# A gated-DeltaNet decoder trunk: where the next head's decays are traced, and weight operations in halves

## The chip, the cores and the metric

The kernel runs on one core of a Trainium2 chip. The core has a matrix engine (TensorE, PE in the profile; PEld is its weight load), a vector engine (VectorE, DVE), an activation engine (ScalarE, ACT), a general engine (GpSimd, POOL), and a sync engine (SP) that here only issues DMAs. Each works through its own queue in order, and semaphores tie the queues together. The metric is the device time of one execution in microseconds.

## The reference

The model has two layers over a sequence of 1024 tokens of width 1024. The first is a gated DeltaNet with 8 heads, the second a sliding-window attention. The change concerns the first layer's heads and the weights of both layers. For each head, in chunks:

```python
q, k, v = ...            # projection, causal convolution of 4 taps, SiLU; q and k normed
g = cumsum(log-decay)    # within a chunk
decay = exp(where(tri, g[c] - g[s], -inf))
lower = where(strict, beta * (k k^T) * decay, 0)
u, w = solve(I + lower, [v * beta, k * beta * exp(g)])
qk = (q k^T) * decay
for each chunk:          # the recurrence, S is 128 x 256
    v_new = u - w S
    o = (q * exp(g)) S + qk v_new
    S = S * exp(g_last) + (k * exp(g_last - g))^T v_new
```

Then o is normed and gated with SiLU(z) and projected by `a_w_out`; a shared K/V projection, the attention layer and its output projection follow. All weights are float32, and norm factors are vectors of length 1024 that multiply the normed input; in the second layer the kernel multiplies them into the weight rows.

## The kernel before

Every product with a weight is made from three products of a faster 32-bit type: a weight block of 128x1024 values is loaded into `wraw`, `whi` is its rounded value, `wlo` = `wraw` - `whi`, and the input is split in the same way into `hh` and `hl`. `weight` (L138) makes 146 of the 148 blocks (two are made apart in `weight_first`), with the subtraction on DVE (L152). For the weights without a norm factor `whi` comes from POOL (L148); for the 36 with one (K/V and the second layer's input weights) POOL first multiplies the raw block by the factor in place (L150) and ACT makes `whi` (L151). `gemm_ct` (L169) runs 24 matmuls per block and half of the tokens (L175, L177, L179).

The first layer goes head by head, with chunks of 128. `head_in(h)` is the projection of one head: k, q and two blocks of v, each in two halves (`ConvBlock.half`), with a SiLU and its sink behind each half. `head_delta(h)` is the head's own chain: the products of keys and queries (L660) with the decays `dm`, an inverse of the triangular matrix by levels of doubling (L716, L720), two corrections in full precision, a merge that ends in the copy of the last quarter into `xt` (ACT, L761), and then the recurrence over the 8 chunks. A chunk of the recurrence has: the product with the state (L787), the row r (DVE, L789), the product with the inverse (PE, L796), its high part (ACT, L798, tile `Z`) and low part (DVE, L799, tile `lh`), the state's update (PE, L807 to L810; DVE, L813), and the state's high part (ACT, L818, tile `X`) and low part (DVE, L819).

`interleave` (L86) runs the chain of head h and, in its gaps, the projection of head h+1 and the gate of head h. This fixes the order of PE, which runs as traced. On the other engines a planner orders the instructions: it issues what is ready, in the order of the trace where several are, so an instruction whose inputs come early can run well ahead of its place in the trace. `keep_in_program_order` ties an instruction to the one traced ahead of it on its engine.

The decays of a head are loaded (`decays_load`, L598), masked on POOL (`decays`, L603) and put through eight exponentials of 128x128 on ACT (L607). `dm` has one buffer for even heads and one for odd heads. The mask and the first exponential are marked with `keep_in_program_order`; the other seven are not. In `head_in`, decays of heads 1 to 7 are traced one tick behind the first half of the first v block; head 0 starts on its own and has them behind the first half of the second. ACT holds one set of function tables at a time; the exponential and SiLU are in different sets, and a table load stands in its queue at each change.

Of the kernel before, what the change touches and what calls it, by code (L numbers as in the profile page):

```python
# [13 lines left out]
ALU = mybir.AluOpType  # L14
# [4 lines left out]
P = 128  # L19
# [45 lines left out]
class Kernel:  # L65
# [72 lines left out]
    def weight(self, src, shape, gain=None):  # L138

        nc = self.nc  # L140
        pool = self.wpools[self.wcount % len(self.wpools)]
        self.wcount += 1
        view = lambda t: t.rearrange("p (k c) -> p k c", k=shape[0])
        raw = self.weight_load(src, shape)
        hi = view(pool.tile([P, 1024], F32R, name="whi"))
        lo = view(pool.tile([P, 1024], F32R, name="wlo"))
        if gain is None:
            nc.gpsimd.tensor_scalar(out=hi, in0=raw, scalar1=1.0, scalar2=1.0, op0=ALU.mult, op1=ALU.mult)  # L148
        else:
            nc.gpsimd.tensor_tensor(out=raw, in0=raw, in1=gain.unsqueeze(2).broadcast_to([P] + shape), op=ALU.mult)  # L150
            nc.scalar.copy(out=hi, in_=raw)  # L151
        nc.vector.tensor_tensor(out=lo, in0=raw, in1=self.f32(hi), op=ALU.subtract)  # L152
        return hi, lo

    def fetch(self):
# [455 lines left out]
    def head_in(self, h, started=None):  # L611
        if started is None:
            k, q, v_sink = self.head_blocks(h)
            self.head_tiles(h)
            H = self.nxt
            self.decays_load(h, H)
            for half in range(2):
                yield from k.half(half)
            for half in range(2):
                yield from q.half(half)  # L620
        else:
            k, q, v_sink = started
            H = self.nxt
        v = [None, None]
        for vb in range(2):
            v[vb] = self.ConvBlock(self, 16 + 2 * h + vb, v_sink(vb))
            for half in range(2):
                yield from v[vb].half(half)
                if (vb, half) == ((0, 0) if started is None else (1, 0)):
                    if started is not None:  # L630
                        self.later(1, lambda: self.decays_load(h, H))
                    self.later(1, lambda: self.decays(h, H))
        self.cur = H

# [761 lines left out]
```

## Time and profile before

| | |
|---|---|
| median of 3 runs | 1904.08 us (1901.43 to 1906.32) |
| profiled execution | 1903.49 us, of which the span is 1901.7 us |
| PE busy | 1831.0 us, 96% of the span |
| DVE busy | 1232.2 us, 65% |
| ACT busy | 813.6 us, 43% |
| POOL busy | 517.1 us, 27% |
| first layer's heads | about 104 to 855 us |
| its output projection | about 855 to 1095 us |
| second layer with attention | about 1095 to 1750 us |
| its output projection | about 1750 to 1902 us |

The profiled execution is the one that all rows come from. A row of the timeline gives the start, the length, engine, line, operation, output<-input and, in brackets, how long the engine sat idle before it and for what. Matmul ends are modelled, so PE's busy time doesn't say how close PE is to its peak; what counts is where it idles and for whom.

### The profile page before, as it was taken

The numbers are of one execution on the slowest core, as the hardware profiler recorded it, in microseconds if no ns is written. First come the engines' busy times: TensorE is split into PE (matmuls) and PEld (weight loads), VectorE is DVE, ScalarE is ACT, GpSimd is POOL, SyncE is SP. The second block draws the span as 40 slices with busy tenths as digits, with TensorE's granted clock in tenths as the row PEclk, the third lists the DMA queues.
The fourth block names the chain that finished last, engine by engine and source line by source line (L and its number), as shares of the span: only waits on it lengthen the run. The fifth ranks groups of instructions, "written<-read, shape, count | busy, mean of one in ns | idle before, by whom it ended". The sixth has DMA issues, their size and how long they took to land.

```text
span 1901.7 us, 33658 instructions
## 1 busy us (share of the span) xinstructions
PE 1831.0 (96%) x13186; PEld 1566.8 (82%) x13186; DVE 1232.2 (65%) x2868; ACT 813.6 (43%) x1948; POOL 517.1 (27%) x545
## 2 busy tenths in 40 slices
PE   6999999999999998999999999999999999999999
PEld 6677777787878776778999998888788788879999
DVE  6677766768585878765445266787786686753432
ACT  6446353535334353523112043557756656771100
POOL 0332222323232223220211222333433333321111
PEclk9999999999999999999999999999999999999999
DMA  4611111111111111122654321111201111226542
GB/s 148 148 37 39 55 35 56 34 56 45 34 57 34 57 34 57 34 84 95 233 181 153 112 89 45 45 30 51 67 29 51 56 40 51 73 73 196 185 172 80
DMA packets 151267, 149.72 MB, mean 79 GB/s; under 512 B 7242, under 2 KB 124484, under 8 KB 151108
## 3 DMA queue, kind: packets, MB, share of 16 engines
q1 hardware_dynamic: 140768, 130.40, 22.0%
q10 hardware_dynamic: 10340, 17.16, 2.8%
q8 instruction: 104, 1.70, 0.4%
q14 instruction: 55, 0.45, 0.1%
HBM read 116.05 MB, written 31.49 MB: 78 GB/s over the span
## 4 chain that ended last, share of the span: by engine, by line
PE 59%; DVE 20%; issue 8%; ACT 6%; POOL 5%; DMA 1%; SPq 0%; POOLq 0%; ACTq 0%; DVEq 0%
PE mm L177 6%; PE mm L175 6%; PE mm L179 6%; PE acc L914 6%; PE acc L913 6%; PE acc L915 6%; DVE acc L489 4%; PE mm L965 3%; PE mm L967 3%; PE mm L966 3%; DVE wlo L152 2%; ACT lsb L1176 2%; PE pv L1207 1%; POOL acc L486 1%; PE sc L796 1%
## 5 line engine op out<-in xcount | busy, mean ns | idle before, releaser
L175 PE MATMUL mm<-hh,whi 128*128 128x512 f32 (+1 forms) x1040 | 427.2, 411 | 2.3 <-ACT hh L241 2.2
L177 PE MATMUL mm<-hl,whi 128*128 128x512 f32 (+1 forms) x1040 | 417.5, 401 | 1.5 <-DVE hl L242 1.5
L179 PE MATMUL mm<-hh,wlo 128*128 128x512 f32 (+1 forms) x1040 | 415.2, 399 | 0.0
L152 DVE TENSOR_TENSOR wlo<-wraw,whi 128x1024 fp32r<-128x1024 f32 x146 | 184.2, 1262 | 245.7 <-POOL whi L148 219.4
L148 POOL TENSOR_SCALAR whi<-wraw 128x1024 fp32r<-128x1024 f32 x110 | 120.3, 1094 | 504.9 <-PE acc L915 246.4
L175 PEld LDWEIGHTS mm<-hh,whi 128*128 128x128 f32 x1040 | 197.6, 190 | 37.5 <-issue 5.0
L179 PEld LDWEIGHTS mm<-hh,wlo 128*128 128x128 f32 x1040 | 197.2, 190 | 36.2 <-issue 4.2
L177 PEld LDWEIGHTS mm<-hl,whi 128*128 128x128 f32 x1040 | 197.6, 190 | 34.4 <-issue 4.2
L965 PE MATMUL mm<-whi,hh 128*128 128x256 f32 x608 | 180.1, 296 | 0.0
L489 DVE SCALAR_TENSOR_TENSOR acc<-u,cw,acc 128x512 f32<-128x512 f32 x192 | 163.3, 853 | 23.9 <-POOL acc L486 21.8
L967 PE MATMUL mm<-whi,hl 128*128 128x256 f32 x608 | 171.9, 283 | 0.0
L966 PE MATMUL mm<-wlo,hh 128*128 128x256 f32 x608 | 171.8, 283 | 0.0
L913 PE MATMUL acc<-whi,hh 128*128 128x256 f32 x512 | 145.0, 283 | 0.0
L914 PE MATMUL acc<-wlo,hh 128*128 128x256 f32 x512 | 144.9, 283 | 0.0
L915 PE MATMUL acc<-whi,hl 128*128 128x256 f32 x512 | 144.9, 283 | 0.0
L1176 ACT ACTIVATE lsb<-lsb,nm 128x128 f32<-128x128 f32 x256 | 99.8, 392 | 64.2 <-DVE se L1172 54.9
L965 PEld LDWEIGHTS mm<-whi,hh 128*128 128x128 f32 x608 | 115.8, 190 | 11.0 <-issue 10.8
L966 PEld LDWEIGHTS mm<-wlo,hh 128*128 128x128 f32 x608 | 115.9, 191 | 0.2
L967 PEld LDWEIGHTS mm<-whi,hl 128*128 128x128 f32 x608 | 115.6, 190 | 0.0
L486 POOL TENSOR_SCALAR acc<-u,cw 128x512 f32<-128x512 f32 x64 | 63.0, 984 | 181.2 <-ACT u L482 166.8
L1180 POOL TENSOR_TENSOR lsb<-lsb,den 128x512 f32<-128x512 f32 x64 | 68.5, 1070 | 152.6 <-ACT pT L1190 51.5
L914 PE MATMUL acc<-wlo,oh 128*128 128x256 f32 x384 | 108.6, 283 | 0.0
(354 smaller groups left out, 4285.1 us busy)
## 6 DMA issues: line engine op xcount, KB each, us to landing
wraw<-in_a_w_in SPq DMA_DIRECT2D x48, 512.0 KB, 3.9
wraw<-in_a_w_out SPq DMA_DIRECT2D x32, 512.0 KB, 3.7
wraw<-in_b_w_in SPq DMA_DIRECT2D x32, 512.0 KB, 4.0
wraw<-in_b_w_out SPq DMA_DIRECT2D x32, 512.0 KB, 3.7
og<-zs SPq DMA_DIRECT2D x32, 256.0 KB, 2.0
ogT<-zs SPq DMA_DIRECT2D x24, 256.0 KB, 2.1
btab<-lt SPq DMA_DIRECT2D x1, 4096.0 KB, 24.1
dm<-gd SPq DMA_DIRECT2D x8, 512.0 KB, 3.6
```

The costliest lines, as they stand in the source:

```text
L152: nc.vector.tensor_tensor(out=lo, in0=raw, in1=self.f32(hi), op=ALU.subtract)
L175: nc.tensor.matmul(ps, hi[:, k, :], hh[:, k, :], start=(k == 0), stop=False)
L177: nc.tensor.matmul(ps, hi[:, k, :], hl[:, k, :], start=False, stop=False)
L179: nc.tensor.matmul(ps, lo[:, k, :], hh[:, k, :], start=False, stop=(k == KT - 1))
L489: nc.vector.scalar_tensor_tensor(out=acc, in0=u[:, t:t + 512], scalar=cw[:, t, blk:blk + 1], in1=acc, op0=ALU.mult, op1=ALU.add)
L913: nc.tensor.matmul(po, oh[:, kk, ts], hi[:, kk, :], start=(k4 + kk + b == 0), stop=False)
L914: nc.tensor.matmul(po, oh[:, kk, ts], lo[:, kk, :], start=False, stop=False)
L915: nc.tensor.matmul(po, ol[:, kk, ts], hi[:, kk, :], start=False, stop=(k4 + kk + b == 7))
L965: nc.tensor.matmul(ps, hh[:, k, ts], hi[:, k % 4, :], start=(k == 0), stop=False)
L966: nc.tensor.matmul(ps, hh[:, k, ts], lo[:, k % 4, :], start=False, stop=False)
L967: nc.tensor.matmul(ps, hl[:, k, ts], hi[:, k % 4, :], start=False, stop=(k == KT - 1))
L1176: nc.scalar.activation(out=L[:, e, :], in_=L[:, e, :], func=AF.Exp, bias=nm[:, e:e + 1], accum_out=den[:, e:e + 1])
```

## The change

Three edits. In `weight`, the subtraction that makes `wlo` is written as two instructions, one for each half of the block, and so is the product with the norm factor on POOL; `whi` is still made in one. In `head_in`, for heads 1 to 7, `decays` is called directly behind the first half of q, instead of one tick behind the first half of the first v block, which lies two halves of a projection later. Head 0 keeps its place, and `decays_load` too.

```diff
+        halves = (slice(0, shape[0] // 2), slice(shape[0] // 2, shape[0]))
         if gain is None:
             nc.gpsimd.tensor_scalar(out=hi, in0=raw, scalar1=1.0, scalar2=1.0, op0=ALU.mult, op1=ALU.mult)
         else:
-            nc.gpsimd.tensor_tensor(out=raw, in0=raw, in1=gain.unsqueeze(2).broadcast_to([P] + shape), op=ALU.mult)
+            for ks in halves:
+                nc.gpsimd.tensor_tensor(out=raw[:, ks], in0=raw[:, ks], op=ALU.mult,
+                                        in1=gain[:, ks].unsqueeze(2).broadcast_to([P, shape[0] // 2, shape[1]]))
             nc.scalar.copy(out=hi, in_=raw)
-        nc.vector.tensor_tensor(out=lo, in0=raw, in1=self.f32(hi), op=ALU.subtract)
+        for ks in halves:
+            nc.vector.tensor_tensor(out=lo[:, ks], in0=raw[:, ks], in1=self.f32(hi[:, ks]), op=ALU.subtract)
         return hi, lo
...
             for half in range(2):
                 yield from q.half(half)
+                if half == 0:
+                    self.decays(h, H)
         else:
             k, q, v_sink = started
...
             for half in range(2):
                 yield from v[vb].half(half)
-                if (vb, half) == ((0, 0) if started is None else (1, 0)):
-                    if started is not None:
-                        self.later(1, lambda: self.decays_load(h, H))
+                if started is not None and (vb, half) == (1, 0):
+                    self.later(1, lambda: self.decays_load(h, H))
                     self.later(1, lambda: self.decays(h, H))
```

## Rows read from the trace of the kernel before

**Rows 1.** The page, part 1: busy us of each engine, instructions

```profile
PE 1831.0 (96%) x13186; PEld 1566.8 (82%) x13186; DVE 1232.2 (65%) x2868; ACT 813.6 (43%) x1948; POOL 517.1 (27%) x545
```

**Rows 2.** PE's waits, whole span: waiter, releaser, total us, times, longest

```profile
PE sc L810 <- DVE lh L799: 8.3, 10, 1.9
PE sc L796 <- ACT xt L761: 6.7, 4, 1.7
...
PE tp L1186 <- POOL lsb L1180: 6.1, 5, 2.7
PE lg L1160 <- DVE m L1166: 4.7, 3, 4.0
PE sc L796 <- DVE r L789: 4.1, 6, 0.8
```

**Rows 3.** Timeline, decays on ACT and POOL, heads 0 and 1: start, us

```profile
102.34 4.50 ACT L607 ACTIVATE dm<-dm,mG 128x128 f32<-128x128 f32 x15
...
152.84 0.40 ACT L607 ACTIVATE dm<-dm,mG 128x128 f32<-128x128 f32 x1
...
150.03 1.09 POOL L603 TENSOR_SCALAR_AFFINE_SELECT dm<-dm 128x1024 f32<-128x1024 f32 x1 [5.25 <-DMA dm<-gd]
```

**Rows 4.** Timeline of head 1, merge to second row, all engines, 244 to 262

```profile
247.28 1.28 ACT L607 ACT_TABLE_LOAD   x1
...
248.58 0.40 ACT L607 ACTIVATE dm<-dm,mG 128x128 f32<-128x128 f32 x1
...
249.00 0.58 ACT L761 COPY xt<-kqp 64x512 f32<-64x512 f32 x1
249.63 0.70 PE L796 MATMUL sc<-vt,xt 128*128 128x256 f32 x2 [1.69 <-ACT xt L761]
249.94 0.34 SPq L598 DMA_DIRECT2D dm<-gd  x1
...
253.67 1.88 POOL L603 TENSOR_SCALAR_AFFINE_SELECT dm<-dm 128x1024 f32<-128x1024 f32 x1
...
255.58 0.99 ACT L607 ACTIVATE dm<-dm,mG 128x128 f32<-128x128 f32 x3 [0.33 <-POOL dm L603]
...
256.27 0.70 PE L796 MATMUL sc<-r,xt 128*128 128x256 f32 x2 [0.83 <-DVE r L789]
...
257.01 0.48 ACT L798 ACTIVATE Z<-sc,beta 128x256 fp32r<-128x256 f32 x1 [0.44 <-PE sc L796]
...
258.32 0.28 PE L807 MATMUL sc<-Z,w 128*128 128x256 f32 x1
...
260.86 0.39 ACT L818 CAST X<-S 128x256 fp32r<-128x256 f32 x1
```

**Rows 5.** Timeline of head 1, ACT in the inverse, 226 to 240

```profile
230.16 0.62 ACT L733 CAST XT<-w 128x512 f16<-128x512 f32 x1 [0.47 <-DVE w L725]
...
238.12 0.64 ACT L534 ACTIVATE kq<-acc 128x512 f32<-128x512 f32 x1 [5.54 <-DVE acc L489]
```

**Rows 6.** Timeline of the second layer, DVE and POOL

```profile
1170.56 0.68 DVE L1089 COPY qr<-mm 128x512 f32<-128x512 f32 x1
...
1171.16 1.22 DVE L152 TENSOR_TENSOR wlo<-wraw,whi 128x1024 fp32r<-128x1024 f32 x1
...
1172.29 0.68 DVE L1092 TENSOR_REDUCE ssqb<-sq 128x8 f32<-128x512 f32 x1
...
1174.34 1.90 POOL L150 TENSOR_TENSOR wraw<-wraw,gcolb 128x1024 f32<-128x1024 f32 x1 [1.04 <-DVE ssqb L115]
...
1174.46 1.81 DVE L117 TENSOR_TENSOR rqbt<-ssqb,rqby 128x16 f32<-128x16 f32 x1
...
1516.07 1.04 POOL L1180 TENSOR_TENSOR lsb<-lsb,den 128x512 f32<-128x512 f32 x1
```

**Rows 7.** Windows of head 6: stretch, us, busy PE, PEld, DVE, ACT, POOL, clock

```profile
755.00:760.00 5.00, 2.62 (x12) 1.72 (x10) 4.97 (x6) 0.74 (x2) 1.36 (x1) 0.96 0.56 162
760.00:765.00 5.00, 4.54 (x13) 3.78 (x14) 3.67 (x7) 2.34 (x6) 0.00 (x0) 0.50 0.47 145
```

## Prediction

> **What bounds the kernel now.** I read four views, from the whole to one spot. The page's busy line first: TensorE (PE) is busy 1831.0 us of the 1901.7 us span [rows 1], so it idles about 71 us, and a change that moves no matmul can win only from those. Then PE's waits over the whole span, longest first [rows 2]: they are scattered, and two belong to the place that the change touches. One is the first product of a head's recurrence (L796) waiting for the copy of the finished inverse on ScalarE (ACT), 6.7 us in four pieces of 1.7. The other is the same line waiting for the vector engine's (DVE's) row update r (L789), 4.1 us in six pieces, the longest 0.8. Third, the decays alone on ACT and GpSimd (POOL) [rows 3]. Last, the timeline of head 1 from the end of its inverse to the second row of its recurrence [rows 4]. Heads 2, 3 and 4 repeat it (the 1.7 us stands four times in the list), so a gain there counts four times.
>
> **What the edit of the decays really moves.** The code traces a mask and eight exponentials per head. The trace shows 15 exponentials in one go from 102.34 (eight of head 0, seven of head 1), and the sixteenth, behind a table load, alone at 152.84 [rows 3]. So seven of eight, and the mask, already run a head ahead of where they are traced, as soon as the decays have landed; only the first exponential, the one kept in program order, stays at its place. The diff therefore moves one exponential per head. The mask and the other seven should stay: their DMA is issued when the head before last has given up its buffer (249.94 in head 1) and the mask follows at 253.67 [rows 4].
>
> **Where it leaves.** Today that exponential and its table load stand on ACT right ahead of the copy of the inverse: load 1.28 from 247.28, exponential 0.40, copy at 249.00, and L796 starts at 249.63 after 1.69 us of idling [rows 4]. Without them ACT is free for the copy at 247.28, 1.72 us sooner, which covers the whole 1.69.
>
> **Where it goes.** Behind the square of the first half of q, which frees ACT at 229.69 in head 1 (0.47 us of idling before 230.16). Load and exponential end near 231.4, so the fp16 copy of 230.16 starts 1.2 us later; no wait of PE for that copy stands in the list, and I cost it at nothing. The table back to SiLU is needed only at 238.12, where ACT had idled 5.54 us [rows 5]: 1.28 hidden. If that cover failed, each load would cost at most its 1.28.
>
> **What is late next.** With PE 1.69 us earlier, the mask still starts at 253.67, as its DMA depends on another chain. It took 1.88 us here against 1.09 where nothing collided [rows 3, 4]. Ahead of it DVE's subtraction and the low part of the state will have finished, so r is in time, the 0.83 us wait of 256.27 goes too, and PE arrives 2.52 us early. But ACT's queue holds three exponentials (0.99) ahead of the next value row (257.01). With an undisturbed mask they run 254.8 to 255.8, and that row ends at 256.3; PE would want it for L807 at 258.32 - 2.52 = 255.8 and waits 0.5 [rows 4]. Behind it stand four exponentials, a table load back and a SiLU before the copy of the state, 3.85 us from row to copy (257.01 to 260.86): that copy comes near 259.65, 1.2 us earlier than now [rows 4]. So 2.0 us survive at L807 and 1.2 at the copy; I take 1.5 per head, nearer to the later of the two, **6.0 us for four heads**. The bounds: a loss of 1.28 x 4 = 5.1, if the added load lands in the chain and both waits stay, and 2.52 x 4 = 10.1 won if no new wait forms. Heads 0, 5 and 6 get nothing: there the row waits for DVE.
>
> **The subtraction in halves.** 146 of these instructions (148 weight blocks, two of them made apart) become 292 of 128x512. One of 1024 lasts 1.22 us and lets the next start after 1.13 (1171.16 to 1172.29); the 512-wide copy before it lets the next start after 0.60 [rows 6]. Two halves thus take 1.20, 0.07 more, about 10 us of DVE over the kernel. DVE is busy 65% of the span [rows 1], and the extra time hides in its gaps and behind the matmuls queued on PE; I cost it at nothing except in heads 5 and 6, where PE does wait for DVE (L810 [rows 2]): 0.4 each, a few of these steps, **0.8 us lost**. Bounds: 1 us won, where an urgent operation goes between two halves, and the whole 10 us lost if that cover is gone.
>
> The Trainium skill speaks against this cut: VectorE: DVE Perf Modes (section on the TRN2 errata) has each instruction pay a fixed cost, 58 cycles in its table and about 150 as measured, so fewer and larger is better. By 150 cycles at 0.96 GHz the cut would cost an estimated 23 us of DVE time instead of 10; the rows above, where starts overlap the tail, bear out the smaller.
>
> **The product in halves.** 36 instructions on POOL of 1.90 us become 72, each near the 1.04 of the 128x512 product, 6.5 us more of an engine that is busy 27% [rows 1, 6]. While one runs, a 128x16 operation on DVE took 1.81 us and ended with it [rows 6]: the loser stands until the other instruction is over. A half holds DVE for half as long, and a softmax product can go between. At stake are PE's waits for the row maximum (4.7 us, one of 4.0) and for the softmax product (6.1 us in five) [rows 2]. Each long one could lose 0.9 to 1.5 us, 3.2 in all; halves also double the number of collisions, so I take **1.9 us won**, between -1 and 3.8.
>
> Sum: 6.0 - 0.8 + 1.9 = 7.1. The profiled execution took 1903.49 us, 1.8 outside its span and 0.6 below the median of the runs: 1903.5 - 7.1 = **1896.4**.
>
> **The rivals.** (a) The stall moves down the same queue. The exponentials now need two loads of their own, Exp and back, for the lone one and for the group of seven. If the load in front of the group starts only with the mask's end (254.8), exponentials run 256.0 to 257.0 and the value row starts at 257.0 as now. Then only part of the 0.83 us by which L807 (258.32) trails that row's end (257.49) is won; with 0.5 per head, 2.0 in all, the time is 1901.5. For it: the fixed order on ACT. Against: the load of 247.28 waited for nothing, and ACT, which idled 0.33 us before the exponentials of 255.58, will be free 1.69 earlier, from 253.6 [rows 4].
>
> The page ScalarE: Activation LUTs (section What ACT_TABLE_LOAD costs) would make this the likely case: it counts 1.28 us and about 1.38 of drain per switch and advises grouping by table. Here the exponential starts at 248.58, 0.02 after the load's end, so the trace shows no drain [rows 4].
>
> (b) Slower, through the clock. In heads 5 and 6 PE idles for DVE (L810, 8.3 us over the kernel [rows 2]), and in head 6, after a slice in which PE was busy 2.62 of 5 us, the granted clock is 0.50 of full speed, that is 1.2 GHz, for the next 5 us [rows 7], which costs 2.5 us of matmul time. DVE's extra instructions and changed turns with POOL lie there. If the halves stretch these waits so that two or three more such slices follow, and ACT's queue gives back the 6 us, the time is 1903.5 + 0.8 + 5.0 to 7.5, about 1910. It decides from the second further drop on: 0.8 + 2 x 2.5 = 5.8 us.
>
> (c) The first exponential doesn't move, or its neighbours follow it: only the halves act, 1902.4.
>
> (d) Both waits stay gone and POOL's halves help everywhere: 10.1 + 3.8, so 1889.6.
>
> **How the numbers follow.** Forecast 0.48, with 1891 to 1900 as its own range; (a) 0.28; (b) 0.10; (c) 0.04; (d) 0.10. A measurement can tell 0.3%, 5.7 us, from no change, so faster means below 1898.4: 0.42 of the forecast and (d), 0.52. Same: the rest of the forecast, (a) and (c), 0.38. Slower: (b), 0.10. The range must reach past (d) and past (a) into the unhidden DVE time: 1888 to 1906.
>
> **What would show it.** Right: in heads 1 to 4 no Exp load between the SiLU and the inverse's copy, L796's wait of 1.69 gone, about five more Exp loads, masks still behind their DMA, and each of the four heads about 1.5 us shorter. Wrong: masks that moved, a longer wait for the value row (L807 on L798), or a second clock drop in heads 5 and 6.

## The result, and the profile after

The changed kernel takes 1892.38 us (median of four runs, 1887.67 to 1894.54) against 1904.62 (median of four, 1901.43 to 1906.32): a ratio of 0.9934, 95% interval 0.991 to 0.9958. By the medians 12.2 us are won, by the interval 8 to 17; the forecast was 7.1 and 1896.4. The execution that was profiled took 1894.54 us with a span of 1892.8, so between the two profiles the gain is 8.9 us of span. The page's busy line of the changed kernel (busy time, share of the span, instructions of each engine):

```profile
PE 1829.7 (97%) x13186; PEld 1567.2 (83%) x13186; DVE 1239.6 (65%) x3014; ACT 838.1 (44%) x1968; POOL 512.6 (27%) x581
```

Against [rows 1], PE's busy time is 1.3 us less and its idle time fell from 71 to 63 us: what was won is waiting. DVE has 146 instructions and 7.4 us more, ACT 20 instructions (all of them table loads) and 24.5 us more. PE's waits over the whole span (who waited for whom: us in total, times, longest), a selection with those that answer to [rows 2] and new ones among them (L816 is the L810 of before, L1192 L1186, L802 L796, L1166 L1160; L694 is a product of the inverse, L688 before):

```profile
PE sc L816 <- DVE lh L805: 12.7, 15, 1.9
PE tp L1192 <- POOL lsb L1186: 5.9, 5, 2.0
PE kqp L694 <- DVE X L726: 2.7, 5, 0.7
PE sc L802 <- DVE r L795: 1.4, 3, 0.6
PE lg L1166 <- DVE m L1172: 0.6, 1, 0.6
PE sc L802 <- ACT xt L767: 0.2, 1, 0.2
```

The wait for the inverse's copy is gone but for 0.2 us (6.7 in [rows 2]), the one for r is a third of what it was, and the wait of 4 us for the row maximum, far from the decays, is 0.6. Of these two grew: the low part of the value row (12.7 against 8.3), and the inverse's wait for DVE at L726, 2.7 us in five pieces. The timeline of head 1, the stretch of [rows 4], in order of time (start, duration, engine, line, idle time before and its releaser):

```profile
231.85 1.28 ACT L612 ACT_TABLE_LOAD   x1
233.14 0.40 ACT L612 ACTIVATE dm<-dm,mG 128x128 f32<-128x128 f32 x1
233.45 0.60 ACT L739 CAST XT<-w 128x512 f16<-128x512 f32 x1
234.74 1.28 ACT L539 ACT_TABLE_LOAD   x1
249.34 0.58 ACT L767 COPY xt<-kqp 64x512 f32<-64x512 f32 x1
...
249.97 0.70 PE L802 MATMUL sc<-vt,xt 128*128 128x256 f32 x2
...
251.97 0.34 SPq L603 DMA_DIRECT2D dm<-gd  x1
...
255.63 0.59 PE L802 MATMUL sc<-r,xt 128*128 128x256 f32 x2
...
255.84 1.51 POOL L608 TENSOR_SCALAR_AFFINE_SELECT dm<-dm 128x1024 f32<-128x1024 f32 x1 [1.97 <-DVE acc L494]
...
257.39 0.40 ACT L612 ACTIVATE dm<-dm,mG 128x128 f32<-128x128 f32 x1 [0.49 <-POOL dm L608]
257.70 0.45 ACT L804 ACTIVATE Z<-sc,beta 128x256 fp32r<-128x256 f32 x1
...
258.20 0.39 PE L813 MATMUL sc<-Z,w 128*128 128x256 f32 x1 [0.45 <-ACT Z L804]
...
258.53 1.28 ACT L575 ACT_TABLE_LOAD   x1
...
259.13 0.38 PE L816 MATMUL sc<-lh,w 128*128 128x256 f32 x1 [0.19 <-DVE lh L805]
...
260.77 1.28 ACT L612 ACT_TABLE_LOAD   x1
```

The lone exponential and its load run at 231.85, between the square of q and the fp16 copy, and a load back to SiLU follows at 234.74. Ahead of the inverse's copy (249.34) there is no exponential any more, and PE starts at 249.97 and 255.63 with no idle time where [rows 4] has 1.69 and 0.83. The mask (255.84) still starts behind its DMA (251.97). Its seven exponentials are now torn apart, one at 257.39 and six behind 260.77, with a SiLU and two table loads between; PE waits 0.45 for the value row at 258.20 and 0.19 at 259.13. The first inverse products of heads 1 to 4 start at 249.97, 354.00, 458.02 and 562.33, so a head takes 104.0 to 104.3 us against 105.36 before (249.63, 354.99, 460.33, 565.70).

At the place of [rows 6] in the second layer (one product on GpSimd in two halves, DVE's norm steps beside it, and PE's product behind the row maximum):

```profile
1171.32 2.04 POOL L153 TENSOR_TENSOR wraw<-wraw,gcolb 128x512 f32<-128x512 f32 x2 [1.68 <-DVE m L1172]
...
1171.56 0.82 DVE L119 SCALAR_TENSOR_TENSOR rqby<-rqbt,rqby 128x16 f32<-128x16 f32 x1
1172.58 0.81 DVE L117 TENSOR_TENSOR rqbt<-ssqb,rqby 128x16 f32<-128x16 f32 x1
...
1172.71 0.39 PE L1166 MATMUL lg<-kh,qT 128*128 128x256 f32 x1 [0.57 <-DVE m L1172]
```

DVE is held 0.8 us at a time and PE waits 0.57. Before, PE waited 3.99 us here (its longest in [rows 2]), and two whole products fell into that one wait: the first held DVE for 1.81 us [rows 6], and the next one, behind it, for 1.70:

```profile
1177.36 1.70 DVE L117 TENSOR_TENSOR rqbt<-ssqb,rqby 128x16 f32<-128x16 f32 x1
```

### The profile page after: what moved, and what is told of

The parts are those of the page before. It is cut to its first block, busy times and chain, and to the rows that moved or that the text cites. A ratio compares the mean times of both kernels' runs of the same rounds, so it can differ in the third digit from the quotient of the medians.

```text
span 1892.8 us, 34012 instructions
## 1 busy us (share of the span) xinstructions
PE 1829.7 (97%) x13186; PEld 1567.2 (83%) x13186; DVE 1239.6 (65%) x3014; ACT 838.1 (44%) x1968; POOL 512.6 (27%) x581
## 4 chain that ended last, share of the span: by engine, by line
PE 68%; DVE 13%; issue 5%; ACT 4%; POOL 3%; DMA 1%; POOLq 0%; ACTq 0%; SPq 0%; DVEq 0%
PE mm L182 8%; PE mm L180 8%; PE mm L184 8%; PE acc L920 6%; PE acc L919 6%; PE acc L921 6%; PE mm L971 4%; PE mm L973 3%; PE mm L972 3%; DVE acc L494 3%; PE pv L1213 2%; DVE wlo L157 2%; PE tp L1192 1%; PE kqp L666 1%; PE lg L1167 1%
## 5 line engine op out<-in xcount | busy, mean ns | idle before, releaser
L157 DVE TENSOR_TENSOR wlo<-wraw,whi 128x512 fp32r<-128x512 f32 x292 | 210.8, 749 | 239.4 <-POOL whi L150 214.0
L919 PE MATMUL acc<-whi,oh 128*128 128x256 f32 x384 | 108.6, 283 | 0.0
L921 PE MATMUL acc<-whi,ol 128*128 128x256 f32 x384 | 108.5, 283 | 0.0
```

What stands on the lines that cost most here:

```text
L157: nc.vector.tensor_tensor(out=lo[:, ks], in0=raw[:, ks], in1=self.f32(hi[:, ks]), op=ALU.subtract)
L919: nc.tensor.matmul(po, oh[:, kk, ts], hi[:, kk, :], start=(k4 + kk + b == 0), stop=False)
L921: nc.tensor.matmul(po, ol[:, kk, ts], hi[:, kk, :], start=False, stop=(k4 + kk + b == 7))
```

## The experiments

All kernels were compared with the kernel before on the same chip. "Won" is (1 - ratio) x 1904.5. From one execution to the next, the stretches in which PE is granted 1.2 GHz differ in number, which moves a run by several us. The last column takes that out: each run's time times its own mean granted clock, averaged, against the same of the kernel before (1894.7 to 1895.2 in every set, and 1894.9 for the changed kernel, in whose own set the clocks of before are not recorded). In the largest set, 28 runs of before, the spread of single runs falls from 2.5 to 1.2 us by it, in the smaller ones by less; by the spread that is left, the column is good to 1 to 2 us. It also takes out what an edit itself wins or loses in clock: the mean is 0.9965 in e9_quarters and 0.9967 in e10_noprod against 0.9949 of before in the same set, and whether that is chance or the edit isn't shown.

| kernel | differs from before in | median us | ratio, 95% interval | won | won, clock taken out |
|---|---|---|---|---|---|
| changed | all three edits | 1892.38 | 0.9934 [0.991, 0.9958] | 12.6 | 11.2 |
| e1_decays | decays | 1897.75 | 0.9972 [0.9962, 0.9983] | 5.3 | 5.6 |
| e2_subtract | subtraction in halves | 1905.57 | 1.0008 [0.9997, 1.0019] | -1.5 | 0.3 |
| e3_product | product in halves | 1899.05 | 0.9972 [0.9961, 0.9983] | 5.3 | 4.5 |
| e4_pin8 | all three, eight exponentials kept in order | 1893.98 | 0.9948 [0.993, 0.9965] | 9.9 | 10.7 |
| e5_unpinned | all three, no exponential kept in order | 1890.94 | 0.993 [0.9912, 0.9947] | 13.3 | 10.3 |
| e6_halves | subtraction and product | 1898.51 | 0.9965 [0.9953, 0.9977] | 6.7 | 4.3 |
| e7_no_sub | decays and product | 1890.32 | 0.992 [0.9908, 0.9933] | 15.2 | 12.9 |
| e8_sub_part | decays, product, subtraction in heads 5 to 7 | 1886.7 | 0.9905 [0.989, 0.992] | 18.1 | 15.9 |
| e9_quarters | product in quarters | 1895.48 | 0.9949 [0.9936, 0.9963] | 9.7 | 6.4 |
| e10_noprod | product left out | 1889.0 | 0.9913 [0.9898, 0.9929] | 16.6 | 12.4 |
| e11_part_pin8 | e8, eight exponentials kept in order | 1887.47 | 0.9902 [0.9886, 0.9918] | 18.7 | 17.8 |
| e12_part_quarters | e8, product in quarters | 1886.81 | 0.9905 [0.9888, 0.9922] | 18.1 | 16.3 |

Where it was won is read by a second means. PE runs its instructions in nearly one order in all these kernels, so they can be matched one by one between two traces. The lead is the start before minus the start in the other kernel, in us, with half of every stretch at 1.2 GHz up to there taken out of both. At six of PE's instructions, named by their starts in the trace of before:

| kernel | head 1, L796 at 249.6 | head 4, L796 at 565.7 | end of the heads, L520 at 812.9 | seam of the layers, L234 at 1104.4 | behind the row maximum, L1161 at 1180.2 | L966 at 1600.0 |
|---|---|---|---|---|---|---|
| changed | 1.4 | 5.1 | 6.6 | 3.8 | 6.6 | 8.9 |
| e1_decays | 2.4 | 8.1 | 7.2 | 5.5 | 6.5 | 5.7 |
| e2_subtract | -2.2 | -2.6 | 1.1 | -1.4 | 1.1 | 1.0 |
| e3_product | 0.4 | 0.4 | 0.8 | 0.7 | 1.8 | 5.6 |
| e7_no_sub | 3.6 | 9.3 | 7.2 | 7.1 | 8.9 | 11.9 |
| e8_sub_part | 2.9 | 8.7 | 10.6 | 9.9 | 11.0 | 14.7 |
| e10_noprod | 0.4 | 0.5 | 0.3 | 0.9 | 4.1 | 11.9 |
| e11_part_pin8 | 3.0 | 11.4 | 14.3 | 14.1 | 15.0 | 19.1 |

Each lead is that of one execution. At the end of the heads e3_product, e10_noprod and e9_quarters (not in the table) have only run what the kernel before runs too, and their leads read 0.8, 0.3 and -0.9: a lead is good to about 1 us.

### One part at a time

Each of these is the kernel before with the lines of the diff for one part and nothing else: the two of head_in, the subtraction's loop, or the product's loop.

> The kernel before with the edit of the decays alone: products and subtractions stay whole. Theory of the forecast: the lone exponential with its table load leaves its place ahead of the copy of the inverse, each of heads 1 to 4 loses about 1.3 to 1.5 us of PE's waiting (1.69 at the first inverse product and 0.83 at the second gone, about 1.0 given back at the value row and the low part), so 5 to 6 us less than the kernel before, near 1899. If the added table loads took it back, the time would be within 2 us of before. If the edit only works together with shorter DVE and POOL operations beside it, the gain is under 3 us and the 0.83 us wait is still there in every head.

5.3 us were won, as forecast. Of PE's waits in this kernel these matter here (L811 waits for the value row's low part, L1187 is the softmax product's reader, L1161 waits for the row maximum):

```profile
PE sc L811 <- DVE lh L800: 11.2, 15, 1.9
PE tp L1187 <- POOL lsb L1181: 6.6, 7, 2.7
PE lg L1161 <- DVE m L1167: 4.9, 3, 3.8
PE tr L234 <- DVE xo L227: 1.9, 2, 1.2
PE sc L797 <- DVE r L790: 1.4, 3, 0.6
```

The wait for the copy isn't in the list at all, and of r's 4.1 us [rows 2] 1.4 are left. The lead grows by 5.7 us from head 1's first inverse product to head 4's, 1.9 a head. In each of heads 1 to 4 it gains 1.5 to 1.9 us at the wait for the copy and 0.9 at the wait for r, and gives back 0.4 at the value row (L808) and 0.5 at its low part (L811). It gives back 0.9 more in heads 5 to 7, which is within the error of a lead, and 1.7 at the seam (the wait for xo above, 1.9 us), and nothing of the second layer's waits is gained: m is still 4.9 us.

> The kernel before with the subtraction in halves alone. Theory of the forecast: 7 us more of DVE, nearly all hidden, 0.8 us slower (between 1 us faster and 10 slower). Rival: the halves are what shortens the second layer, since an urgent DVE operation no longer stands behind 1.2 us: 2 to 5 us faster, with PE's 4 us wait for the row maximum gone.

The interval includes no difference at all, as the forecast had it, but it didn't come about as pictured. The lead falls to -2.2 by head 1, is -2.6 at head 4, rises to 1.1 by the end of the heads, loses 2.5 up to the seam and wins 2.5 at the row maximum. Two of its waits:

```profile
PE kqp L691 <- DVE X L723: 2.7, 5, 0.7
PE sc L799 <- DVE r L792: 2.0, 6, 0.4
```

The wait at L691 (five of 0.5 to 0.7 us, one in each of heads 0 to 4) is new. DVE's timelines show its origin. First the kernel with the subtraction whole (e7_no_sub), then the changed kernel, at the same place in head 1's inverse:

```profile
215.87 1.23 DVE L156 TENSOR_TENSOR wlo<-wraw,whi 128x1024 fp32r<-128x1024 f32 x1 [0.55 <-POOL whi L150]
217.01 0.69 DVE L725 TENSOR_TENSOR X<-kqp,X 128x512 f16<-128x512 f32 x1
```

```profile
217.63 0.69 DVE L157 TENSOR_TENSOR wlo<-wraw,whi 128x512 fp32r<-128x512 f32 x1 [0.56 <-POOL whi L150]
218.84 0.75 DVE L494 SCALAR_TENSOR_TENSOR acc<-u,cw,acc 128x512 f32<-128x512 f32 x1 [0.52 <-POOL acc L491]
219.50 0.68 DVE L726 TENSOR_TENSOR X<-kqp,X 128x512 f16<-128x512 f32 x1
```

Whole, the subtraction is followed at once by the inverse's X (L725 there, L726 in the changed kernel), which ends 1.83 us after the subtraction's start. In halves, a convolution step stands between them, DVE idles 0.52 us until GpSimd has its input ready, and X ends 2.55 us after the first half's start, with the other half still to come. The cut gave DVE's order another turn, not only shorter pieces. In heads 1 to 4 of e2_subtract that is paid back: the wait for r (L799) is 2.0 us where [rows 2] has 4.1, about 0.5 less a head. Beside the decays' edit, which empties the wait for r by itself, only the loss is left: the changed kernel falls behind e7_no_sub by another 2.0 us from head 1 to head 4 (leads of 1.4 and 5.1 against 3.6 and 9.3).

> The kernel before with the product in halves alone, in both layers. Theory of the forecast: 1.9 us faster (1 slower to 3.8 faster). What the changed kernel's trace suggests is more: PE's 3.99 us wait for the row maximum is down to 0.57 there, and PE is 6 us further ahead at the second layer's end than at its start; if all of that is the product's, this kernel is 4 to 6 us faster. Rival: that gain is the subtraction's or only a shift of phase, and this kernel is within 2 us of before with a wait of over 3 us for the row maximum.

5.3 us were won (4.5 with the clock taken out), between the forecast's 1.9 and the upper end of what the changed kernel's trace suggested. The lead is still 0.7 at the seam and 5.6 at the end, so all of it lies in the second layer. Every step of more than 0.3 us in the lead there stands at one of two of PE's waits, for the row maximum (1.0, 0.9 and 0.5 won) or for the softmax product (0.6 lost, then 0.3, 1.8 and 0.9 won). The two waits in all:

```profile
PE tp L1190 <- POOL lsb L1184: 4.7, 5, 2.9
PE lg L1164 <- DVE m L1170: 3.3, 2, 2.9
```

The row maximum's went from 4.7 us [rows 2] to 3.3, the softmax product's from 6.1 to 4.7; the longest stay at 2.9.

### Two parts at a time

e6_halves leaves out the diff's lines in head_in; e7_no_sub leaves out the subtraction's loop.

> The kernel before with both cuts, subtraction and product, and the decays where they were. If the parts add, as measured alone (subtraction 1.5 us slower, product 5.3 faster): 3.8 us faster, near 1900.7. If the two cuts help each other in the second layer (PE's wait for the row maximum there went from 3.99 us to 2.89 with the product cut alone, to 1.38 with the subtraction cut alone, to 0.57 with all): 6 to 8 us faster, near 1897.5.

6.7 us, where the parts alone give 5.3 - 1.5 = 3.8; with the clock taken out 4.3, where they give 4.8. The two cuts about add; that they help each other by 3 us is not borne out.

> The changed kernel with the subtraction whole: decays and products alone. If the parts add: 5.3 + 5.3 = 10.6 us faster than before, near 1894, 1 to 2 us from the changed kernel. If the cut of the subtraction is worth something only beside the other two, as the changed kernel's 12 us against the sum of 9 would have it: 1895 to 1898.

Faster than either theory had it: 15.2 us, where the parts add to 10.6; with the clock taken out 12.9 against 10.1. By the lead at 1600 us, one execution of each, it is 11.9 against 11.3, so the size of the surplus is open. Part of the difference shows at the seam, where e1_decays gives back 1.7 us of lead and this kernel none. GpSimd's product and DVE's subtraction there, first in e1_decays and then in e7_no_sub (start, duration):

```profile
1083.71 1.90 POOL L150 TENSOR_TENSOR wraw<-wraw,gcolb 128x1024 f32<-128x1024 f32 x1 [2.87 <-DMA wraw<-in_w_kv]
...
1083.89 2.79 DVE L152 TENSOR_TENSOR wlo<-wraw,whi 128x1024 fp32r<-128x1024 f32 x1 [4.81 <-ACT whi L151]
1086.61 2.47 DVE L920 TENSOR_TENSOR xo<-acc,xo 128x512 f32<-128x512 f32 x4
```

```profile
1083.70 3.13 POOL L153 TENSOR_TENSOR wraw<-wraw,gcolb 128x512 f32<-128x512 f32 x2 [2.63 <-DMA wraw<-in_w_kv]
...
1083.70 1.23 DVE L156 TENSOR_TENSOR wlo<-wraw,whi 128x1024 fp32r<-128x1024 f32 x1 [4.53 <-ACT whi L155]
1084.84 1.30 DVE L924 TENSOR_TENSOR xo<-acc,xo 128x512 f32<-128x512 f32 x2
```

With the whole product, GpSimd started 0.18 us ahead and DVE's subtraction took 2.79; four sums of the output projection piled up behind it and began at 1086.61. With halves both started at 1083.70, the subtraction took 1.23, GpSimd needed 3.13 for its two pieces, and the sums began at 1084.84. From there to the norm's factors and PE's transposes the steps are the same. The Trainium skill's page SBUF — State Buffer (section SBUF: two separate sides) has an operation of DVE with two inputs in SBUF and one of GpSimd exclude each other for the whole of whichever starts first; the trace agrees: the product ends at 1085.61, and the subtraction 1.07 us later, at 1086.68. The changed kernel has the seam's loss again (6.6 to 3.8 in the table, chiefly at PE's two waits for xo, 1.9, and one for `wlo` at 926 us, 1.2). So the cut of the whole subtraction is worth nothing beside the other two, and rather costs 2 us (1892.38 against 1890.32; 11.2 against 12.9), though the intervals overlap.

### The exponentials' place and their table loads

```diff
# e4_pin8: the changed kernel with
-            if n == 0:
-                tc.keep_in_program_order(e)
+            tc.keep_in_program_order(e)
# e5_unpinned: the changed kernel without the first two of these lines
```

> The changed kernel with all eight exponentials of a head kept in the order of the code, behind the square of the first half of q, in place of the first alone. If the split group costs (two further table loads and seven exponentials between the rows of the recurrence, with PE waiting 0.45 us for the value row and 0.2 to 0.7 for its low part in each head), those waits go and each of heads 1 to 4 gains about 1 us more: near 1888, with about 10 table loads for the exponentials in place of 20. Rival: the eight exponentials (2.6 us with 1.28 of load) then stand ahead of the fp16 copy of the inverse, its product waits for them, and the time is the changed kernel's or up to 4 us more.

> The changed kernel without the line that keeps the first exponential in the order of the code. Theory: what the edit of the decays won is that the lone exponential no longer stands ahead of the copy of the inverse, and its new place costs nothing; free, it joins its seven neighbours behind the mask, a head ahead, with about 10 to 16 table loads in place of 20, PE's 1.69 us wait for the copy stays gone, and the time is the changed kernel's within 3 us. Rival: the place in the inverse itself matters (the group in the rows then has eight exponentials, the value row waits longer), 4 us or more slower than the changed kernel.

Table loads in front of the exponentials (L612) and SiLUs, in the changed kernel and then in e4_pin8 (the number behind x is what counts):

```profile
L612 ACT ACT_TABLE_LOAD x20 | 25.7, 1283 | 0.4
L575 ACT ACT_TABLE_LOAD x14 | 18.0, 1283 | 0.3
L539 ACT ACT_TABLE_LOAD x7 | 9.0, 1283 | 1.4 <-DVE dml L646 1.3
```

```profile
L612 ACT ACT_TABLE_LOAD x8 | 10.3, 1283 | 0.1
L575 ACT ACT_TABLE_LOAD x2 | 2.6, 1283 | 0.0
L539 ACT ACT_TABLE_LOAD x7 | 9.0, 1283 | 1.4 <-DVE dml L645 1.3
```

Before there were 10 for the exponentials and 11 at the value blocks' SiLU, 21 in all. The changed kernel has 41 of these loads, e4_pin8 17, e5_unpinned 27 (13 and 14), and their times lie within 3 us of each other, at 10.3 to 11.2 us won with the clock taken out. In e4_pin8 the waits at the value row did go and the lead at the heads' end is 7.8 against 6.6, but its time isn't lower: the expected 4 us didn't come. Free of its order, the first exponential leaves the copy of the inverse as well, and the time is the same. So what the decays' edit won is the place that the exponential left; neither the new place nor the added loads cost anything that these three kernels can show.

### The subtraction cut in part

```diff
-        for ks in halves:
+        for ks in halves if 36 <= self.wcount <= 48 or self.wcount >= 83 else (slice(0, shape[0]),):
             nc.vector.tensor_tensor(out=lo[:, ks], ...
```

> The changed kernel with the subtraction cut only where the trace of the kernel with that cut alone gained on PE: weight blocks 36 to 48 (heads 5 to 7) and from 83 on (second layer); whole elsewhere (heads 0 to 4, where PE fell back by some 5 us, and the first output projection). Theory: the cut's loss and gain are separate places, so this is faster than the changed kernel by 2 to 5 us, near 1888. Rival: those losses and gains are shifts of phase that come back elsewhere, and the time is the changed kernel's within 2 us.

The edit does less than the expectation says. `wcount` isn't the number of the block in the kernel: the code sets it back to 1 ahead of the first output projection, and to 0 ahead of the second layer and of the last projection, so it never reaches 83. The page's busy line shows it, with 14 instructions on DVE more than the 2868 of [rows 1]:

```profile
PE 1828.4 (97%) x13186; PEld 1565.5 (83%) x13186; DVE 1228.8 (65%) x2882; ACT 838.2 (44%) x1968; POOL 520.0 (28%) x581
```

14 blocks are cut: 13 between 611 and 862 us, which is heads 5 to 7, and a single one of the second layer, at 1666 us. The other 132 are whole, in this kernel and in the two below that carry the same line.

18.1 us faster than before (15.2 to 20.9) and 5.7 below the changed kernel's median. By the lead it is 3.6 us ahead of the changed kernel at head 4, 4.0 at the heads' end, 6.1 at the seam and 5.8 at 1600 us. Against e7_no_sub, which has the whole subtraction everywhere, it wins 3.4 us up to the heads' end and is still 2.8 ahead at 1600 us (15.9 against 12.9 with the clock taken out). So what the cut loses and wins are places, not phases that come back: it wins in heads 5 to 7 and loses ahead of them. What it would be worth in the second layer beside the cut product no kernel here tests by itself; from the seam to 1600 us the changed kernel, which has it there, wins 5.1 us of lead, and e8_sub_part and e7_no_sub, which don't, win 4.8 each.

> The kernel with the subtraction cut only in heads 5 to 7 and in the second layer, and all eight exponentials kept behind the square of the first half of q. With all eight there the changed kernel's waits at the value row went but its time didn't; if it is the cut subtraction in heads 0 to 4 that made those waits, nothing more is to be had: within 2 us of 1886.7. If the table loads between the rows cost by themselves: 2 to 4 us faster, near 1884.

Here too the subtraction is cut in heads 5 to 7 only. The same median, though its profiled execution has a lead 3.7 us greater at the heads' end. With the clock taken out it is 1.9 us ahead of e8_sub_part, which the intervals of the two don't separate; whether the loads between the rows cost those 2 us stays open.

### What the product costs in all

```diff
# e9_quarters: the kernel before with
+        quarters = [slice(i * shape[0] // 4, (i + 1) * shape[0] // 4) for i in range(4)]
+            for ks in quarters:
+                nc.gpsimd.tensor_tensor(out=raw[:, ks], in0=raw[:, ks], op=ALU.mult, ...
# e10_noprod: the kernel before without
-            nc.gpsimd.tensor_tensor(out=raw, in0=raw, in1=gain.unsqueeze(2)..., op=ALU.mult)
```

> The kernel before with the product alone, cut in quarters (128x256 each). Theory: what the product costs PE is the time for which one piece holds DVE out, so a shorter piece helps further; the wait for the row maximum, 3.99 us whole and 2.89 in halves, falls below 2.5, and the whole kernel is 6 to 8 us faster than before, 1 to 3 more than with halves. Rival: the number of collisions doubles again and eats this, or the gain of the halves came from DVE's changed order alone: within 2 us of the halves (5 us faster) or behind them.

> The kernel before without the product: the second layer's weights are left without their norm factor, the rest is unchanged. This is the whole price of the product. Theory: GpSimd's hold on DVE is what costs, and with it gone both the row maximum's wait (4.9 us in three) and most of the softmax product's (6 to 7 us) go: 8 to 11 us faster than before, so halves win about half of all that is to be had. Rival: the halves already took it all: 5 to 6 us.

Without any product 16.6 us are won (12.4 with the clock taken out), more than either side of its expectation, with quarters 9.7 (6.4), with halves 5.3 (4.5). By the lead, 11.0 of the 11.9 us that e10_noprod has won at 1600 us stand at PE's waits for the row maximum and the softmax product, so it is these waits that the product costs. The waits for the softmax product and the row maximum in e9_quarters, and for the softmax product in e10_noprod:

```profile
PE tp L1190 <- POOL lsb L1184: 4.4, 4, 1.6
PE lg L1164 <- DVE m L1170: 2.4, 2, 2.0
```

```profile
PE tp L1185 <- POOL lsb L1179: 1.5, 1, 1.5
```

The row maximum's longest wait is 3.99 whole, 2.9 in halves, 2.0 in quarters; the softmax product's 6.1 us in all becomes 1.5 without the product. For these waits the length of one hold counts more than the number of holds: the number doubled twice and the waits fell both times. For the time of the kernel that is less sure: with the clock taken out quarters are 1.9 us ahead of halves, which the rival (within 2 us) allows too.

> The kernel with the subtraction cut only in heads 5 to 7 and in the second layer (18 us faster than before), and the product in quarters in place of halves. Theory: shorter holds of GpSimd on DVE help here as they did alone (quarters 9.7 us faster than before, halves 5.3; without the clock's share 6.4 against 4.5): 2 to 4 us faster again, near 1883, the fastest of all. Rival: the cut subtraction has already freed DVE's turns in the second layer, and quarters only add collisions: within 2 us of 1886.7 or slower.

Within 0.1 us of e8_sub_part's median (16.3 against 15.9 with the clock taken out): here quarters bring nothing over halves. The rival's reason, a cut subtraction in the second layer, can't be the cause, as it is whole there in both kernels (all but one block). So that quarters are worth more than halves is not confirmed. The fastest kernels of the study are e8_sub_part, e11_part_pin8 and this one, which can't be told apart.

## Why the prediction was right, and where it was not

The forecast of 1896.4 lies 4.0 us above the measured median; 1892.38 is inside its own range of 1891 to 1900. The largest part of the difference is one term, the product. By its steps:

**What moves.** Right: one exponential a head, with mask and DMA where they were. Not foreseen: the other seven were torn apart by a SiLU, so that ten more Exp loads came, not five, and ten more back.

**Where it leaves and where it goes.** Right on both: the 1.69 us is gone in all four heads, the load and exponential end at 233.54, and the fp16 copy slips by 1.1 us (233.45 against 230.16, of which 2.2 are the lag that the changed kernel has there already) with no wait of PE for it.

**What is late next.** The size is near, 5.3 us measured alone against 6.0, and so is the kind: two new waits, at the value row (0.45 against 0.5 forecast) and behind it. The detail was wrong: the mask took 1.51, not 1.09, one exponential instead of three stood ahead of the row, and the second wait is for the row's low part (L816, 0.19), not for the copy of the state. In e1_decays a head won 1.9 against the 1.5 forecast; in the changed kernel, where a head is 1.1 to 1.3 shorter, the cut subtraction took the rest (L694, and the low part at L816). So four heads alone won 7 to 8 us, above the forecast, and heads 5 to 7 and the seam, for which nothing was forecast, gave 2.6 back: by luck the sum is nearer than its parts.

**The subtraction in halves.** The sum is right (0.8 lost forecast; between 1.5 lost and 0.3 won), the place is not. It was priced as a loss in heads 5 and 6; there it won (lead -2.6 to 1.1 over heads 5 to 7 in e2_subtract), and the loss lies up to head 1 and at the seam, and beside the decays' edit in each of heads 1 to 4 too. "Costed at nothing except in heads 5 and 6" is the sentence that failed, and two errors cancelled. DVE's busy time rose by 10.0 us in e2_subtract, as forecast (7.4 in the changed kernel, where the halved products hold it less: by themselves, in e3_product, they take 5.6 off DVE's busy time), far from the 23 that the Trainium skill's page VectorE: DVE Perf Modes (section on the TRN2 errata) would give: the trace decides for the row's smaller figure.

**The product in halves.** This is the term that was mis-sized: 1.9 forecast with 3.8 as its upper end, 5.3 measured (4.5 with the clock taken out). The mechanism was right, the two waits named are where the lead of e3_product moves, and the stake was right too: 4.7 and 6.1 us [rows 2], against 11.0 won at these waits in e10_noprod. What failed is the part of it that halves take. The sizing counted "each long one", 3.2 us in all, and took off 1.3 for more collisions. The lead of e3_product shows six gains, four of 0.9 to 1.8 us and two of 0.3 and 0.5, against one loss of 0.6, 4.8 in sum. The 4 us wait that the prediction counts as one collision held two. The cost on GpSimd came out as forecast: the products took 81.7 us in 72 pieces against 75.3 in 36, 6.4 more against 6.5.

**The rivals.** (a), whose 1901.5 leaves out the 1.1 us of the two cuts, fell: a head won 1.1 to 1.3 us, not 0.5, and 17, 27 or 41 loads made no difference. The Trainium skill's page ScalarE: Activation LUTs (section What ACT_TABLE_LOAD costs), by which each switch costs 1.28 us and a drain, is borne out for the 1.28 of ACT's own time (24.5 us for 20 loads); no drain shows (the exponential at 233.14 starts 0.01 behind its load's end), and the kernel's time shows neither. (b) fell: the mean granted clock is 0.995 against 0.996, and over heads 5 and 6 (665 to 770 us) it is 0.97 against 0.95. (c) fell with the 1.69. (d), with 1889.6, is a little nearer to the measured time than the forecast: it was right that the halves win more than 1.9 (its 3.8 still falls short), and that both waits of the heads stay gone, and wrong that no new wait forms behind them.

**The sum.** 5.3 - 1.5 + 5.3 = 9.1 (10.4 with the clock taken out) against 12.6 (11.2): within what the intervals allow, so the parts about add in the changed kernel. By the leads at 1600 us they give more than it has, 5.7 + 1.0 + 5.6 = 12.3 against 8.9, but its profiled execution is the slowest of its four, by 1.4 us behind their mean with the clock taken out. In e7_no_sub the parts fall short by 3 to 5 us of time (0.6 of lead); of that only the 1.7 at the seam has been traced, and the rest stays open.

## What to carry over

When two engines exclude each other, price the longest single hold and every place where one stands behind it, not the total of either engine's work; leaving the work out for one run shows what is at stake. Cutting an instruction in halves also gives the order another turn, so cut it only in the stages where someone waits behind it and look at each stage for what moved in between. When an edit is meant for some stages only, count in the trace which instructions it reached: here a counter that starts again left the second layer out. Compare changes of under 1% with the clock's share taken out beside the plain times, and by where one engine's instructions stand, not by medians alone.

## What the runs showed of the chip

With 17, 27 and 41 table loads of 1.28 us each on ACT, the kernels that differ in the exponentials' place alone took 1893.98, 1890.94 and 1892.38 us: the loads made no difference to the time that could be told. ACT is idle over half of the span in all three; that this is the reason wasn't tested. A GpSimd instruction and a DVE instruction that exclude each other change places by as little as 0.2 us: at the seam product and subtraction took 1.90 and 2.79 us one way round, 3.13 (two pieces) and 1.23 the other. The number of stretches at 1.2 GHz varies between executions of one kernel, and explains half of the spread of its times in the largest set (2.5 to 1.2 us).
